# A two-layer decoder trunk on one core: every probability tile transposed by DMA, its halves parted and joined on ScalarE, VectorE and GpSimd

## The chip, the core and the metric

The kernel runs on one core of one Trainium2 chip. A core has TensorE (PE in the profile, with PEld for its weight loads), VectorE (DVE), ScalarE (ACT), GpSimd (POOL) and SyncE (SP, which only issues DMAs). Each engine executes its own instructions in a fixed order and waits for the others by semaphores. The metric is the time of one execution in device microseconds, lower is better.

## The reference

The input x is 256 tokens x 1024 features, float32. Two layers, each an attention mixer and a SwiGLU feed-forward of width 2816, with RMS norms between:

```python
for i in range(DEPTH):                       # DEPTH = 2
    if i % 2 == 0: h = h + dilated_mixer(rmsnorm(h, a_norm), a_w_in, a_w_out)
    else:          h = h + forgetting_mixer(rmsnorm(h, b_norm), b_w_in, b_f, b_w_out)
    h = h + swiglu(rmsnorm(h, ffn_norm[i]), ffn_w_gu[i], ffn_w_down[i])
return rmsnorm(h, final_norm)
```

The first attention (`dilated_mixer`) has 16 heads of 64 features and three groups of query, key and value projections: group 0 sees the last 128 tokens, groups 1 and 2 every 4th and every 16th token. The outputs of the three are mixed by their softmax denominators, which amounts to one softmax over all three groups' scores. The second (`forgetting_mixer`) is causal attention over all 256 tokens with a bias from a learned decay. In both, probabilities p and values v meet as `p @ v`.

## The kernel before

TensorE multiplies in a reduced-precision float32 format. Each operand is therefore kept as a high and a low part (ScalarE rounds the high part, VectorE subtracts it, `split` at L80 and L84), and `mm3` does every product as three matmuls (L203, L208). The weights come from HBM in pieces of 1024 columns (`raw`, issued by SP at L101), five in flight, and are split two units of work ahead of their use (`AHEAD = 2`).

A *unit* is one weight matrix of 1024 x 256 times all tokens: 48 matmuls of 256 columns or 24 of 512. Heads are worked in four *quads* (`hq`) of four heads, a quad as two *pairs* (`pr`) of two heads (`h`). The list `a_units` writes the order of the first attention's 36 units out by hand, `b_units` that of the second's 12. `later(i, fn, ...)` puts attention work behind unit i of the list, `due.pop` carries it out there; in the second attention a due time of i - 0.5 is the middle of unit i.

In the first attention a quad goes through `scores_0` and `scores_12` (matmuls into PSUM), `softmax_a`, a transposition of the probabilities (each tile `p` holds 128 queries x 640 keys), and `pv_a`, the products with the values. Quads 0 to 2 transpose with `turn_a`: GpSimd parts each float32 into its two 16-bit halves (L528), SP issues a DMA that transposes the 16-bit blocks (L530), ScalarE joins the halves (L531). Quad 3 uses `trans_a`: TensorE multiplies each 128 x 128 block by the identity (`transposed`, L301), and ScalarE or VectorE copies the result from PSUM (L306). In the second attention all quads use TensorE (`trans_b`, three groups of four blocks): `scores_b` behind unit j, `trans_b` one and a half units later, `pv_b` two units later, where the next quad's `scores_b` stands too. `out_proj` then multiplies the attention's output (`ot`) by the output matrix in *triples* (one `mm3` of 512 columns), for the first 128 tokens and then for the other 128, and takes in what is still due: quad 3's transposition after some triples, its products after more, and after them the triples that need them. The norm of the first 128 tokens (`residual`, `norm_t`) is worked beside the second 128's triples.

`first()` raises the priority of instructions when the order of each engine is laid down; `issue_after` ties that order to an instruction. Buffers are named by tags ("pt", "bias", "xn", "p", "h"), each with a fixed number of slots.

Of the kernel before, what the change touches and what calls it, by code (L numbers as in the profile page):

```python
# [17 lines left out]
P = 128  # L18
# [14 lines left out]
def trunk(ctx: ExitStack, tc: tile.TileContext, T, out):  # L33
# [222 lines left out]
    def v_tile(o=None, r=None):  # L256

        v = ap.tile([P, 512], F32, tag="v", name="v", bufs=7)
        with first():
            if r:  # L260
                for t in range(2):
                    s = slice(t * S, (t + 1) * S)
                    nc.scalar.activation(v[:, s], o[:, s], AF.Copy, scale=r[t])
            elif o is not None:
                nc.scalar.activation(v, o, AF.Copy)
        return v
# [27 lines left out]

    copied = {}

    def transposed(blocks, copy=nc.vector.tensor_copy, tag="tr", home="pt"):

        tr = psum(tag)
        for i, b in enumerate(blocks):  # L300
            nc.tensor.transpose(tr[:, i * P:(i + 1) * P], b, ident)  # L301
        n = len(blocks) * P
        bufs, cols = {"pt": (3, 640), "bias": (4, 6 * P)}[home]
        w = ap.tile([P, cols], F32, tag=home, name="pt", bufs=bufs)
        with first():
            copied["last"] = copy(w[:, :n], tr[:, :n])  # L306
        return w
# [157 lines left out]
    def scores_12(quad):  # L465

        sc = [psum("sc") for _ in range(2)]
# [42 lines left out]
    def trans_a(quad, pr):  # L510

        pt = quad["pt"]
        block = lambda h, i: pt[pr, h][:, i * P:(i + 1) * P]
        home = ("pt", "bias")[pr]
        quad["w", pr] = [transposed([block(h, 1 + qb) for h in range(2) for qb in range(2)], nc.scalar.copy, home=home),
                         transposed([block(h, 3) for h in range(2)], home=home),
                         transposed([block(h, b * 4) for h in range(2) for b in range(2)], nc.scalar.copy, "o", home)]

    def turn_a(quad, pr):

        quad["w", pr] = []
        bufs = {"pt": 3, "bias": 4}
        parts = lambda x: x[:, :640].bitcast(U16).rearrange("p (c t) -> p t c", t=2)
        for h in range(2):
            home = ("pt", "bias")[pr]
            w = ap.tile([P, 640 if home == "pt" else 6 * P], F32, tag=home, name="pt", bufs=bufs[home])
            split16 = w[:, :640].bitcast(U16)
            nc.gpsimd.tensor_copy(split16.rearrange("p (t c) -> p t c", t=2), parts(quad["pt"][pr, h]))  # L528
            turned = ap.tile([P, 6 * P], F32, tag="bias", name="turned", bufs=4)[:, :640].bitcast(U16)
            nc.sync.dma_start_transpose(turned.rearrange("p (g c) -> p g c", c=P), split16)  # L530
            nc.scalar.copy(parts(w), turned.rearrange("p (t c) -> p t c", t=2))  # L531
            quad["w", pr].append(w)

    def pv_a(quad, pr):
        vs, ws = quad["v"], quad["w", pr]
        o = psum("o")
        if len(ws) == 2:
            blocks = [w[:, :640].rearrange("p (i j) -> p i j", j=P) for w in ws]
            straight = lambda h: ws[h][:, P:3 * P]
            corner = lambda h: ws[h][:, 3 * P:4 * P]  # L540
            dilated = lambda h, a: blocks[h][:, 0:5:4, a * 32:a * 32 + 32]
        else:
            straight = lambda h: ws[0][:, h * S:(h + 1) * S]
            corner = lambda h: ws[1][:, h * P:(h + 1) * P]
            dilated = lambda h, a: halves(ws[2][:, h * S:(h + 1) * S], a)
        pv(o[:, :S], vs[0], 0, pr, straight, S, True, False)
        pv(o[:, P:S], vs[0], 1, pr, corner, P, False, False)
        halves = lambda x, a: x.rearrange("p (b n) -> p b n", b=2)[:, :, a * 32:a * 32 + 32]
        for a in range(4):
            pv(halves(o[:, :S], a), vs[1 + a % 2], a // 2, pr, lambda h: dilated(h, a), 64, False, a == 3)  # L550
# [10 lines left out]
    for i, (hq, g, w) in enumerate(a_units):  # L561
# [6 lines left out]
        if i != 3 and (w < 2 or g == 0 and hq > 1):  # L568
            o = psum("mm")
# [11 lines left out]
        if w < 2:  # L581
# [26 lines left out]
            if w == 1:  # L608

                j = i + (hq == 0)  # L610
                step = lambda hq: 9 * hq + 11 + 2 * (hq == 0)
                if g == 0:
                    later(step(hq - 1) + 2 if hq else j + 3, scores_0, quad)
                if g == 2:
                    later(j + 1, scores_12, quad)
                    later(j + 1, softmax_a, quad)
                    for pr in range(2):
                        if hq == 3:
                            later(step(hq) + pr, trans_a, quad, pr)
                        else:  # L620
                            later(j + 1, turn_a, quad, pr)
                    for pr in range(2):
                        later(step(hq) + 2, pv_a, quad, pr)
        elif g == 0 and hq > 1:
            for t in range(2):
                proj_tok(xt, wt, o[:, t * S:(t + 1) * S], t)
            quad["v"][0] = v_tile(o, r_a)
# [30 lines left out]
    def out_proj(nm, ot, h, grow, ks, done, banks):  # L658
# [3 lines left out]
        res = []  # L662

        def part(t, acc, nk):
            last = None
            for n, k in nk:
                c = (k % 2) * D + n * 512
                last = mm3(acc[n], both(ot, ALL, k, slice(t * P, (t + 1) * P)),
# [3 lines left out]
        def cols(ks):  # L672
            return [(n, k) for n in range(2) for k in ks]

        for t in range(2):
            acc = [psum(banks[t]) for _ in range(2)]
            if t == 0:

                nk = cols(range(ks))
                last = part(t, acc, nk[:done])  # L680
                nk = nk[done:]
                per = -(-len(nk) // (len(due) - 1))
                for i in sorted(due):
                    with tc.issue_after(last.ins):
                        for fn, a in due[i]:
                            fn(*a)
                    last = part(t, acc, nk[:per]) or last
                    nk = nk[per:]
                due.clear()
                part(t, acc, nk)  # L690
                last = part(t, acc, cols(range(ks, KT)))
            else:
                part(t, acc, cols(range(2)))
                with tc.issue_after(last.ins):
                    part(t, acc, cols(range(2, 6)))
                    norm_t(*res[0], grow, xt, 0)
                    part(t, acc, cols(range(6, KT)))
            res.append(residual(acc, h[t], f"h_{nm}{t}"))
# [114 lines left out]
    hs, xt = out_proj("a_out", ot, x, g_f, 6, 6, ("sc", "mm"))  # L813
# [73 lines left out]
    def scores_b(hq):  # L887
# [9 lines left out]
        for pr in range(2):  # L897
# [13 lines left out]
            release(added)  # L911
# [7 lines left out]
    def trans_b(hq):  # L919
        pt = bq[hq]["pt"]  # L920
        square = lambda pr: [pt[pr, h][:, qb * P:(qb + 1) * P] for h in range(2) for qb in range(2)]
        w = [transposed(square(0)), transposed([pt[pr, h][:, 2 * P:3 * P] for pr in range(2) for h in range(2)]),
# [216 lines left out]
```

## Time and profile before

| | |
|---|---|
| median of 3 runs | 736.82 us (735.57 to 736.84) |
| profiled execution | 736.1 us, its span 734.3 us |
| granted TensorE clock | 0.997 |
| PE busy | 726.4 us (99%) |
| DVE busy | 495.9 us (68%) |
| ACT busy | 388.7 us (53%) |
| POOL busy | 83.0 us (11%) |
| DMA | 141.93 MB, 193 GB/s on average |

The span runs from the first instruction's start to the last one's end. The first attention takes about the first 240 us of it, the first feed-forward the time to about 430, the second attention to about 540. In a row of the timeline stand start, duration, engine, source line, operation, output <- inputs, shape and how many like instructions are merged; in brackets the idle time before it and what ended it. In a row of groups stand the count, the busy time, the mean in ns, and the idle time before. Matmuls overlap, so what one of them costs is read from start to start, not from its duration.

### The profile page before, as it was taken

Reading aid. Unit: us, or ns where it says so; the run is one execution under the profiler, and the core shown is the slowest. Engines: PE = TensorE matmul, PEld = TensorE weight load, DVE = VectorE, ACT = ScalarE, POOL = GpSimd, SP = SyncE. Lnnn points to the kernel's source line nnn. Section 1 sums busy time; section 2 is a strip of 40 time slices with the busy share of each in tenths; the row PEclk is TensorE's granted clock in tenths of the full one; section 3 lists DMA queues with packets and bytes.
Section 4 is the critical chain, followed back from the end, with each engine's and each line's share of the span. In section 5 each row is a group of like instructions: output and inputs, shape, how many; then the busy total and the mean of one; then the engine's idle time right before and its main releaser. Section 6 shows DMA issues by size and latency. Waiting matters only on the chain.

```text
span 734.3 us, 14310 instructions
## 1 busy us (share of the span) xinstructions
PE 726.4 (99%) x5856; PEld 672.4 (92%) x5856; DVE 495.9 (68%) x762; ACT 388.7 (53%) x617; POOL 83.0 (11%) x118
## 2 busy tenths in 40 slices
PE   9999999999999999999999999999999999999996
PEld 7999989999988899999999989999889999999995
DVE  6997998998996775554555474576776554556533
ACT  7646747738445663444554453587475444545421
POOL 0600206007105000000000004110010000000001
PEclk9999999999999999999999999999999999999998
DMA  9865955956864376656567352874547656656601
GB/s 335 306 202 174 237 182 153 289 193 152 268 194 160 116 241 221 195 179 203 195 202 247 127 168 90 294 260 138 172 142 237 222 179 203 195 188 218 198 1 58
DMA packets 55042, 141.93 MB, mean 193 GB/s; under 512 B 20257, under 2 KB 21441, under 8 KB 54977
## 3 DMA queue, kind: packets, MB, share of 16 engines
q1 hardware_dynamic: 54832, 140.88, 59.4%
q8 instruction: 46, 0.75, 0.4%
q14 instruction: 20, 0.16, 0.1%
q10 hardware_dynamic: 144, 0.15, 0.1%
HBM read 136.00 MB, written 1.07 MB: 187 GB/s over the span
## 4 chain that ended last, share of the span: by engine, by line
PE 97%; DVE 1%; ACT 1%; POOL 0%; issue 0%; POOLq 0%; DVEq 0%; ACTq 0%
PE ps_mm L208 34%; PE ps_mm L203 17%; PE ps_tr L208 9%; PE ps_sc L208 8%; PE ps_o L208 7%; PE ps_tr L203 5%; PE ps_sc L203 4%; PE ps_o L203 4%; PE ps_o L313 2%; PE ps_sc L395 2%; PE ps_tr L196 1%; PE ps_tr L301 1%; PE ps_sc L476 1%; PE ps_o L322 1%; PE ps_sc L894 0%; PE ps_sc L458 0%
## 5 line engine op out<-in xcount | busy, mean ns | idle before, releaser
L80 ACT ACTIVATE wh<-raw 128x1024 fp32r<-128x1024 f32 x236 | 243.4, 1054 | 207.1 <-PE ps_tr L208 66.7
L84 DVE TENSOR_TENSOR wl<-raw,wh 128x1024 fp32r<-128x1024 f32 x236 | 288.3, 1242 | 82.6 <-ACT wh L80 82.4
L203 PE MATMUL ps_mm<-xt,wh 128*128 128x256 f32 x816 | 227.2, 279 | 0.2 <-ACT v L281 0.2
L208 PE MATMUL ps_mm<-xt,wl 128*128 128x256 f32 x816 | 226.0, 277 | 0.0
L208 PE MATMUL ps_mm<-xt,wh 128*128 128x256 f32 x816 | 226.0, 277 | 0.0
L203 PEld LDWEIGHTS ps_mm<-xt,wh 128*128 128x128 f32 x816 | 153.1, 188 | 2.2 <-issue 1.7
L208 PEld LDWEIGHTS ps_mm<-xt,wl 128*128 128x128 f32 x816 | 153.6, 188 | 0.1
L208 PEld LDWEIGHTS ps_mm<-xt,wh 128*128 128x128 f32 x816 | 153.4, 188 | 0.0
L208 PE MATMUL ps_tr<-xt,wh 128*128 128x256 f32 x304 | 83.9, 276 | 0.0
L208 PE MATMUL ps_tr<-xt,wl 128*128 128x256 f32 x304 | 83.9, 276 | 0.0
L203 PE MATMUL ps_tr<-xt,wh 128*128 128x256 f32 x304 | 83.7, 276 | 0.0
L730 DVE TENSOR_TENSOR sa<-ps_tr,sa 128x256 f32<-128x256 f32 x38 | 16.1, 424 | 73.5 <-PE ps_tr L208 73.5
L208 PEld LDWEIGHTS ps_tr<-xt,wh 128*128 128x128 f32 x304 | 57.1, 188 | 0.0
L208 PEld LDWEIGHTS ps_tr<-xt,wl 128*128 128x128 f32 x304 | 57.0, 188 | 0.0
L203 PEld LDWEIGHTS ps_tr<-xt,wh 128*128 128x128 f32 x304 | 57.0, 188 | 0.0
L203 PE MATMUL ps_mm<-wh,xt 128*128 128x512 f32 (+1 forms) x144 | 49.8, 346 | 0.0
L173 POOL TENSOR_SCALAR rs<-ssq 128x1 f32<-128x1 f32 x7 | 1.9, 271 | 420.6 <-ACT junk L182 420.6
L208 PE MATMUL ps_mm<-wl,xt 128*128 128x512 f32 (+1 forms) x149 | 49.1, 335 | 0.0
L208 PE MATMUL ps_mm<-wh,xt 128*128 128x512 f32 (+1 forms) x149 | 49.1, 335 | 0.0
L285 POOL COPY v<-v 32x256 f32<-32x256 f32 x64 | 40.5, 632 | 71.2 <-ACT v L281 68.6
L203 PE MATMUL ps_sc<-wh,ah 128*128 128x512 f32 x80 | 31.4, 392 | 0.0
L208 PE MATMUL ps_sc<-wl,ah 128*128 128x512 f32 (+1 forms) x82 | 31.3, 385 | 0.0
(232 smaller groups left out, 1113.6 us busy)
## 6 DMA issues: line engine op xcount, KB each, us to landing
raw<-in_gu SPq DMA_DIRECT2D x88, 512.0 KB, 4.8
raw<-in_a_in SPq DMA_DIRECT2D x68, 512.0 KB, 5.0
raw<-in_dn SPq DMA_DIRECT2D x44, 512.0 KB, 4.7
raw<-in_b_in SPq DMA_DIRECT2D x24, 512.0 KB, 5.0
raw<-in_a_out SPq DMA_DIRECT2D x8, 512.0 KB, 5.0
raw<-in_b_out SPq DMA_DIRECT2D x8, 512.0 KB, 4.4
bias<-sums SPq DMA_DIRECT2D x8, 384.0 KB, 6.6
grow<-in_norms SPq DMA_DIRECT2D x4, 512.0 KB, 5.7
```

Of the source, the lines that this page charges most:

```text
L80: a = nc.scalar.activation(view(hi), src, AF.Copy)
L84: return nc.vector.tensor_tensor(view(lo), src, view(hi).bitcast(F32), op=ALU.subtract)
L196: nc.tensor.transpose(tr[:, k * P:(k + 1) * P], xn[:, kk * P:(kk + 1) * P], ident)
L203: nc.tensor.matmul(o, sh, mh, start=start, stop=False)
L208: last = nc.tensor.matmul(o[:, u], s, m[:, u], start=False, stop=end and u.stop == n)
L285: nc.gpsimd.tensor_copy(v[1 + a % 2][n:n + 32, a // 2 * S:a // 2 * S + S], by_t[a * 32:a * 32 + 32, t, g])
L301: nc.tensor.transpose(tr[:, i * P:(i + 1) * P], b, ident)
L313: nc.tensor.matmul(o[h * HD:(h + 1) * HD], v[:, c:c + HD], w(h), start=start, stop=stop)
L322: nc.tensor.matmul(o[:, :n], mhalf.to_broadcast([P, P]), mhalf.to_broadcast([P, n]), start=True, stop=True)
L395: nc.tensor.matmul(lead[t], xt[y][:, k, t * P:(t + 1) * P], w[z][:, u], start=k + y + z == 0, stop=k == KT - 1 and z == 1)
L476: nc.tensor.matmul(sc[h][c, o:o + 64], q[HR[h], pr, qb * P + a * 32:qb * P + a * 32 + 32], k[HR[h], pr].rearrange("p (b n) -> p b n", b=2) ...
L730: nc.vector.tensor_tensor(a, u, sg, op=ALU.mult)
```

## The change

- Quad 3 of the first attention and all quads of the second take the DMA path; `trans_a`, `trans_b` and `transposed` are gone. For quad 3 of the first attention, pair 0 is parted on GpSimd and joined on ScalarE, pair 1 is parted and joined on VectorE. In the second attention one DMA turns a pair's two heads (1536 halves); pair 0 is parted on GpSimd, pair 1 on VectorE, and head 0 of each is joined on ScalarE, head 1 on VectorE.
- The parts and joins of all quads are now issued under `first()`.
- In the second attention `pv_b` of quads 0 and 1 comes half a unit later than before, quad 2 and 3's in the output projection; quad 3's `scores_b` comes half a unit earlier.
- In the first attention the group-0 values of quads 2 and 3 are projected together, as the last two units (24 matmuls of 512 columns each), and `pv_a` of quad 2 moves into the output projection with quad 3's. Quad 3's two scores stand together, in different PSUM banks.
- `out_proj` has one written order for both: of the first 128 tokens the triples of quads 0 and 1, then four triples of the other tokens, then quad 2's, then quad 3's; due work comes in after triples 4 and 16 (first attention) or 8 and 16 (second).
- `release` (weight splits held back behind the softmax) comes after pair 1, not after each pair; the splits that waited for a transposition's copy no longer do.

```diff
-        a_units += ([(0, 0, 2), (1, 0, 2)], v12, [(hq, 0, 2)] + v12, v12 + [(hq, 0, 2)])[hq]
+        a_units += ([(0, 0, 2), (1, 0, 2)], v12, v12, v12 + [(2, 0, 2), (3, 0, 2)])[hq]
...
-        sc = [psum("sc") for _ in range(2)]
+        sc = [psum("sc" if quad["hq"] < 3 else "o") for _ in range(2)]
...
+    def parted(x):
+        return x.bitcast(U16).rearrange("p (c t) -> p t c", t=2)
...
     def turn_a(quad, pr):
...
+        last = quad["hq"] == 3
+        if last and pr == 0:
+            quad["room"] = [(hrow(f"apart{h}")[:, :640], p_tile(640)) for h in range(2)]
         for h in range(2):
...
+                own = last and pr == 1
+                (nc.vector if own else nc.gpsimd).tensor_copy(apart.rearrange("p (t c) -> p t c", t=2), parted(p))
...
+                nc.sync.dma_start_transpose(turned.rearrange("p (g c) -> p g c", c=P), apart)
+                (nc.vector.tensor_copy if own else nc.scalar.copy)(parted(w), turned.rearrange("p (t c) -> p t c", t=2))
...
-                    later(step(hq - 1) + 2 if hq else j + 3, scores_0, quad)
+                    later((j + 3, 15, 22, 32)[hq], scores_0, quad)
...
-                        later(step(hq) + 2, pv_a, quad, pr)
+                        later((15, 22, 40, 41)[hq], pv_a, quad, pr)
...
+        cols = lambda t, *ks: [(t, n, k) for i in ks for n in range(2) for k in (2 * i, 2 * i + 1)]
+        head = cols(0, 0, 1) + cols(1, 0) + cols(0, 2)
+        last = None
+        for i, item in enumerate(head + [None]):
+            if i in at:
                 with tc.issue_after(last.ins):
+                    for fn, a in due.pop(min(due)):
+                        fn(*a)
+            if item:
+                last = part(item)
+        last = part(*cols(0, 3))
+        res = [residual(accs[0], h[0], f"h_{nm}0")]
+        with tc.issue_after(last.ins):
+            part(*cols(1, 1, 2))
+            norm_t(*res[0], grow, xt, 0)
+            part(*cols(1, 3))
...
-            release(added)
+            if pr:
+                release(added)
...
+    def turn_b(hq, pr):
+
+        b = bq[hq]
+        w = b["w", pr] = b["bias", pr] if hq == 3 else turn_tile()
+        apart = w.bitcast(U16).rearrange("p (h t c) -> p h t c", h=2, t=2)
+        for h in range(2):
+            with first():
+                (nc.gpsimd, nc.vector)[pr].tensor_copy(apart[:, h], parted(b["pt"][pr, h][:, :3 * P]))
+        with first():
+            turned = ap.tile([P, D], F32, tag="xn", name="turned", bufs=2)[:, :6 * P].bitcast(U16)
+            nc.sync.dma_start_transpose(turned.rearrange("p (g c) -> p g c", c=P), w.bitcast(U16))
+            turned = turned.rearrange("p (h t c) -> p h t c", h=2, t=2)
+            for h in range(2):
+                (nc.scalar.copy, nc.vector.tensor_copy)[h](parted(w[:, h * 3 * P:(h + 1) * 3 * P]), turned[:, h])
...
-                later(j, scores_b, hq)
+                later(j - (hq == 3) / 2, scores_b, hq)
+                for pr in range(2):
+                    later(j - (hq == 3) / 2, turn_b, hq, pr)
+                for pr in range(2):
+                    later((7.5, 9.5, 13, 14)[hq], pv_b, hq, pr)
...
-                later(j + 1.5, trans_b, hq)
-                for pr in range(2):
-                    later(j + 2, pv_b, hq, pr)
```

More of the change, by code (lines that the diff above doesn't have):

```diff
@@ L254, in p_tile, with v_tile @@
         return ap.tile([P, 640], dtype, tag="p", name=name, bufs=6)[:, :n]
-    def v_tile(o=None, r=None):
+    def v_tile(o=None):
         v = ap.tile([P, 512], F32, tag="v", name="v", bufs=7)
[L259 to L264, printed above, removed]
+        if o is not None:
+            with first():
                 nc.scalar.activation(v, o, AF.Copy)
@@ L293, in masked @@
             nc.vector.scalar_tensor_tensor(s, sc, HD ** -0.5, mask, op0=ALU.mult, op1=ALU.add)
[L295 to L307, printed above, removed]
     def pv(o, v, kb, pr, w, n, start, stop):
@@ L524, in turn_a @@
         for h in range(2):
[L525 to L530, printed above, removed]
@@ L531, in turn_a @@
-            nc.scalar.copy(parts(w), turned.rearrange("p (t c) -> p t c", t=2))
+            p = quad["pt"][pr, h]
+            with first():
+                apart, turned = quad["room"][h] if last else (home(("pt", "bias")[pr]), None)
+                w = p if last else apart
+                apart = apart.bitcast(U16)
+                own = last and pr == 1
+                (nc.vector if own else nc.gpsimd).tensor_copy(apart.rearrange("p (t c) -> p t c", t=2), parted(p))
+                if not last:
+                    turned = home(("bias", "pt")[pr * (h == 0)])
+                turned = turned.bitcast(U16)
+                nc.sync.dma_start_transpose(turned.rearrange("p (g c) -> p g c", c=P), apart)
+                (nc.vector.tensor_copy if own else nc.scalar.copy)(parted(w), turned.rearrange("p (t c) -> p t c", t=2))
@@ L567, in trunk @@
             wt = weights("a_in", hq * 9 + g * 3 + w, read if i > 4 else None)
-        if i != 3 and (w < 2 or g == 0 and hq > 1):
+        if i != 3 and w < 2:
             o = psum("mm")
@@ L617, in trunk @@
                     for pr in range(2):
[L618 to L621, printed above, removed]
+                        later(j + 1, turn_a, quad, pr)
                     for pr in range(2):
-                        later(step(hq) + 2, pv_a, quad, pr)
[L624 to L627, printed above, removed]
+                        later((15, 22, 40, 41)[hq], pv_a, quad, pr)
         elif i > 1:
@@ L656, in residual, with out_proj, part @@
         return hn, parts
-    def out_proj(nm, ot, h, grow, ks, done, banks):
+    def out_proj(nm, ot, h, grow, at, banks):
         ws = [weights(nm, i) for i in range(4)]
         xt = xt_tile()
-        res = []
-        def part(t, acc, nk):
+        accs = {}
+        def part(*items):
             last = None
-            for n, k in nk:
+            for t, n, k in items:
+                if t not in accs:
+                    accs[t] = [psum(banks[t]) for _ in range(2)]
                 c = (k % 2) * D + n * 512
-                last = mm3(acc[n], both(ot, ALL, k, slice(t * P, (t + 1) * P)),
+                last = mm3(accs[t][n], both(ot, ALL, k, slice(t * P, (t + 1) * P)),
@@ L699, in out_proj @@
+        res.append(residual(accs[1], h[1], f"h_{nm}1"))
         return res, xt
@@ L967, in trunk @@
             continue
-        lows = [] if any(fn is trans_b for fn, _ in due.get(i - 0.5, ())) else None
-        wt = weights("b_in", hq * 3 + w, behind if i in (3, 5) else lows, hold=held)
+        wt = weights("b_in", hq * 3 + w, behind if i in (3, 5) else None, hold=held)
         o = psum("mm")
@@ L976, in trunk @@
                         fn(*a)
-                    for low in lows or ():
-                        low(copied["last"])
             if w == 0:
@@ L1002, in trunk @@
                         fn(*a)
-                    for low in lows or ():
-                        low(copied["last"])
             bq[hq][w] = v_tile(o)
```

75 lines of the change are left out of this document (17 added, 58 removed).

## The prediction

> **What bounds the kernel now.** I read the page first: busy times, then the chain that ended last.
>
> ```profile
> span 734.3 us, 14310 instructions
> PE 726.4 (99%) x5856; PEld 672.4 (92%) x5856; DVE 495.9 (68%) x762; ACT 388.7 (53%) x617; POOL 83.0 (11%) x118
> PE 97%; DVE 1%; ACT 1%; POOL 0%; issue 0%; POOLq 0%; DVEq 0%; ACTq 0%
> ```
>
> TensorE is busy 99% of the span and is 97% of the chain, so a matmul taken away is time won, as long as nothing that replaces it makes TensorE wait. The profiled execution took 736.1 us, 0.7 below the median of 736.8; a change under 0.2% of that, 1.5 us, can't be told from none.
>
> The unit of cover is read from the timeline of PE: first and last of the 48 matmuls of one unit of 256 columns.
>
> ```profile
> 220.08 0.28 PE L203 MATMUL ps_mm<-wh,xt 128*128 128x256 f32 x1
> 225.41 0.28 PE L208 MATMUL ps_mm<-wh,xt 128*128 128x256 f32 x1
> ```
>
> 47 steps in 5.33 us are 0.113 us a matmul, 5.44 us a unit.
>
> **What goes: the transposes on TensorE.** The same timeline, one group of the first attention and the group of one head quad in the second:
>
> ```profile
> 229.63 0.81 PE L301 MATMUL ps_tr<-ident,p 128*128 128x128 f32 x6
> 230.29 0.60 PE L301 MATMUL ps_o<-ident,p 128*128 128x128 f32 x4
> 230.64 0.48 PE L203 MATMUL ps_sc<-wh,oth 128*128 128x512 f32 x1
> ...
> 525.60 1.03 PE L301 MATMUL ps_tr<-ident,p 128*128 128x128 f32 x8
> 526.47 0.60 PE L301 MATMUL ps_o<-ident,p 128*128 128x128 f32 x4
> 526.82 0.48 PE L203 MATMUL ps_mm<-wh,oth 128*128 128x512 f32 x1
> 527.14 0.40 PE L208 MATMUL ps_mm<-wl,oth 128*128 128x512 f32 x1
> 527.37 0.40 PE L208 MATMUL ps_mm<-wh,otl 128*128 128x512 f32 x1
> ```
>
> Start to start, a matmul of 512 columns takes 0.23 us (527.14 to 527.37), the first after a group 0.32. Ten transposes hold PE from 229.63 to 230.64, with 0.09 for the slow restart 1.10 us; twelve hold it from 525.60 to 526.82, with 0.09 1.31 us. Removed are two groups of ten (quad 3, first attention) and four of twelve: 2 x 1.10 + 4 x 1.31 = **7.44 us**.
>
> **What comes back on TensorE.** Before, a quad's products with the values stand right before the next quad's scores; half a unit later they are a stretch of their own. Three such joints are cut in the second attention. A stretch costs its entry and exit:
>
> ```profile
> 528.76 0.40 PE L208 MATMUL ps_mm<-wh,otl 128*128 128x512 f32 x1
> 529.09 1.52 PE L313 MATMUL ps_o<-pt,v 128*64 128x256 f32 x16
> 530.54 0.50 PE L203 MATMUL ps_mm<-wh,oth 128*128 128x512 f32 x1
> 530.87 0.40 PE L208 MATMUL ps_mm<-wl,oth 128*128 128x512 f32 x1
> ```
>
> 0.33 in place of 0.23 on both sides: 0.2 a stretch, **+0.6 us** for three (0 to 0.6, since two kinds of work side by side may cost a step too). In the first attention the count stays: quad 3's two scores are joined, quad 2's products are parted from them. The products themselves take 1.45 us as before. The values of group 0, quads 2 and 3, become 48 matmuls of 512 columns for 96 of 256: 48 x 0.23 against 96 x 0.113, both 10.9 us, nothing.
>
> **The new path of a probability tile** is part (copy by 16-bit halves), transpose on SP's queue, join (copy back). Three quads of the first attention take it already:
>
> ```profile
> L530 SPq DMA_TRANSPOSE turned<-pt x12: 1267/1366/1601, 73.8 to 185.0; - x12
> L531 ACT COPY pt<-turned x12: 1647/1672/1698, 77.5 to 188.5; 128x1280 uint16<-128x1280 uint16 x12
>   DMA turned<-pt: 14.5, 8
> DMA to landing us min/median/max: 3.3/3.5/5.8
> L528 POOL COPY pt<-p x12: 1247/1358/2245, 72.2 to 183.4; 128x1280 uint16<-128x1280 uint16 x12
> ```
>
> In the second attention one transfer holds two heads, 1536 halves, and each copy 768. By length: a part on POOL 0.6 x 1358 = 0.82 us, a join on ACT 1.0, the transfer 3.5 to 1.2 x 3.5 = 4.2, taken 3.9. A DVE copy of this kind isn't in the trace: 348 ns for 256 elements (row below) gives 1.04 for 768 as the high end, half of that the low one; I take 0.9 for the load and 0.8 in the chain. A handover adds 0.3.
>
> The trace says: landing 3.5 us. [...]
>
> **Is the path covered?** Quad 0 of the second attention has the longest softmax, quad 3 the shortest distance to the end. Chain view, then VectorE and ScalarE timelines:
>
> ```profile
> 472.17 0.66 PE ps_tr L894 x8
> 518.75 0.66 PE ps_tr L894 x8
> ...
> 479.41 0.61 DVE L916 TENSOR_SCALAR p<-p,c_b 128x256 f32<-128x256 f32 x2
> 525.48 0.62 DVE L916 TENSOR_SCALAR p<-p,c_b 128x256 f32<-128x256 f32 x2
> ...
> 479.80 0.68 ACT L915 ACTIVATE p<-p,c_b 128x128 f32<-128x128 f32 x2
> 481.34 0.68 ACT L915 ACTIVATE p<-p,c_b 128x128 f32<-128x128 f32 x2
> ```
>
> Quad 0: scores end at 472.83; pair 0 is ready 7.7 us later (480.48), pair 1 9.2 (482.02), perhaps 1.2 earlier because `release` no longer stands between the pairs. Pair 0: 7.7 + 1.6 + 3.9 + 0.3 + 1.0 = 14.5. Pair 1: 9.2 + 1.6 + 3.9 + 0.3 + 1.0 = 16.0. The products come after units 6 and 7, the next scores (1.5) and half of unit 8: 2.5 x 5.44 + 1.5 = 15.1, pair 1 another 0.7 later, 15.8. So a wait of 0.2, and with the transfer at its high end 0.5: **+0.4**. Quads 1 and 2 have 16.5 us and more. Quad 3: scores end 519.41, pair 1 ready 6.7 later (526.10), joined at 13.5; cover half a unit 2.7, sixteen column triples 16 x 0.68 = 10.9, quad 2's products 1.8: 15.4. Hidden, with 2 us left.
>
> Quad 3 of the first attention: its dilated scores take 1.6, then come 3 units (16.3), sixteen triples (10.9) and quad 2's products (2.38 in the chain and an entry, 2.7): 31.5 us of cover. Quad 2 needed, by the chain and the timeline of ACT,
>
> ```profile
> 158.25 1.41 PE ps_sc L476 x91
> 198.08 2.38 PE ps_o L313 x48
> ...
> 188.49 1.67 ACT L531 COPY pt<-turned 128x1280 uint16<-128x1280 uint16 x1 [6.85 <-DMA turned<-pt]
> ```
>
> 158.25 to 190.16, 31.9 us, with four parts on POOL among sixteen value copies; its products began at 198.08, so nothing waited. Quad 3 leaves two parts there and has two on VectorE, so I take it as hidden; 0.4 is the other end. Quad 2's products, moved behind all units, need nothing late but the values of the last unit, four triples (2.7 us) before.
>
> The output projections' order: after the last product of the first half, norm transposes have eight triples (5.4 us) of cover for twelve.
>
> ```profile
> 533.62 0.69 DVE L654 TENSOR_TENSOR h_b_out<-ps_mm,hf 128x512 f32<-128x512 f32 x1 [0.69 <-PE ps_mm L208]
> 536.08 1.41 DVE L191 SCALAR_TENSOR_TENSOR xn<-h_b_out,rs,grow 128x512 f32<-128x512 f32 x2 [0.70 <-POOL rs L176]
> ```
>
> That chain takes 533.62 to 537.49, 3.9 us: hidden, 1.5 left; without cover it would cost the difference. Weights are needed later than before there, which pays for VectorE's four added copies in quad 3.
>
> **Load of the copying engines**, second attention (stage table 470 to 530, its last line) and the groups of lines:
>
> ```profile
> sum 60.00, PE 60.00 PEld 54.57 DVE 44.71 ACT 42.49 POOL 5.83; mean PE 10.00 PEld 9.09 DVE 7.45 ACT 7.08 POOL 0.97
> ...
> L306 DVE COPY pt<-ps_tr 128x512 f32<-128x512 f32 x8 | 5.2, 686 | 6.1 <-PE ps_tr L301 6.0
> L916 DVE TENSOR_SCALAR p<-p,c_b 128x256 f32<-128x256 f32 x16 | 4.9, 348 | 0.1
> ```
>
> DVE loses 12 evictions (x 0.686 = 8.2; the row groups eight of them) and gains 8 parts and 8 joins (16 x 0.9 = 14.4): 50.9 us. ACT gains 8 joins: 50.5. POOL gains 8 parts, 6.6, and stays idle. PE's stretch becomes 60 - 5.2 + 0.6 = 55.4. Both copying engines go above 90%, and their queues stand still while a join at the head waits for its transfer: 14.5 us over 12 transfers before, 1.2 each, 9.7 for eight. 50.9 + 9.7 is 5.2 too much. The weights are split two units ahead (10.9 us), which absorbs it, but eviction and softmax lose some room: I take **+0.8** (0 to 5.2). Tightest is quad 3: its scores now stand in the middle of the last unit, so the eviction of its keys (512 columns, about the 0.69 of the L306 row) has half a unit, 2.7 us, instead of a whole one; a join at the head of ScalarE that waits over 2 us is paid by TensorE there. On SP the transfers hold back the weight loads behind them by up to their wait for a part; all of that lies in the same lead. `release` after pair 1 delays weight splits by four short VectorE operations, in the lead too.
>
> **Sum.** 736.1 - 7.44 + 0.6 + 0.4 + 0.8 = 730.5; against the median 731.2 us. One more uncertainty: ten microseconds of like matmuls hold 87 or 91 of them,
>
> ```profile
> 120.00:130.00 10.00, 10.00 (x87) 10.00 (x86) 10.00 (x14) 7.96 (x9) 8.06 (x8) 1.00 0.55 102
> 180.00:190.00 10.00, 10.00 (x91) 10.00 (x90) 9.80 (x13) 3.15 (x3) 6.03 (x7) 1.00 0.44 116
> ```
>
> at a full granted clock (1.00) with no wait; 4% over some 30 us, so +-1 us if it changes.
>
> **Rivals.** *The queues don't absorb it* (chance 0.16): the 5.2 us above falls on TensorE in full. 736.8 - 6.8 + 5.2 = 735.2, or anything between. For it: 91% load. Against: the first attention has DVE at 10.00 of 10 in the rows above and PE never stops.
>
> *VectorE stands behind its joins* (slower, 0.13). Its eight joins each hold the queue for a transfer that is late because SP was behind a blocked weight load. With 55.4 - 50.9 + 10.9 = 15.4 us of room, it decides from 1.9 us a join; at 4 us, 32 - 15 = 17 us stall: 736.8 - 6.8 + 17 = 747. It is slower than before from 2.8 us a join ((15.4 + 6.8) / 8). For it: a wait of 6.85 in the row above. Against: the mean of 1.2. GpSimd's parts push the same way: weight splits took
>
> ```profile
> 165.81 1.19 DVE L84 TENSOR_TENSOR wl<-raw,wh 128x1024 fp32r<-128x1024 f32 x1
> 170.88 3.87 DVE L84 TENSOR_TENSOR wl<-raw,wh 128x1024 fp32r<-128x1024 f32 x2 [0.85 <-ACT wh L80]
> ```
>
> 1.94 us each beside POOL copies, 1.19 without. [...]
>
> *Hidden anyway* (0.07): gains and waits cancel within 0.2%, 735.3 to 738.3. Against: PE's transposes are on the chain.
>
> **How the numbers follow.** My forecast of 729 to 733 has 0.64, a part of the 5.2 us (733 to 735.3) 0.16; together faster 0.80, same 0.07, slower 0.13. Low end: all waits 0, no new stretches, matmul pace 1 us better: 736.8 - 7.4 - 1 = 728.4. High end: the first rival in full, 735.2, and the pace 1 us worse: 736.2. Between them lie some 8 in 10.
>
> **What would show it.** No L301 rows; PE busy some 6 us less; around each quad's products no PE gap above 0.5 us. Wrong if PE waits for a join (DVE or ACT, `pt<-turned`) before L313, or if weight splits come late to L203 in the second attention; if DVE's 768 copies take over 1.04 us; or if landings rise above 4.2.

## The result and the profile after

The changed kernel takes 747.01 us (median of four runs; the kernel before, timed beside it, 736.2): ratio 1.0148, 95% interval 1.0126 to 1.0169. The forecast was 731.2, the range 728.4 to 736.2; the sign was wrong. The profiled execution took 745.77 us. Its page, the lines that answer to those of before:

```profile
span 743.8 us, 14168 instructions
PE 724.7 (97%) x5742; PEld 665.5 (89%) x5742; DVE 505.9 (68%) x768; ACT 396.6 (53%) x623; POOL 89.0 (12%) x128
PE 72%; DVE 11%; ACT 5%; DMA 5%; issue 4%; POOL 1%; POOLq 0%; SPq 0%; DVEq 0%; ACTq 0%
```

The transposes are gone, but TensorE is 72% of the chain and not 97%: it waits now. The table by stage shows where. First before, then after; the rows are the first attention and the second, the columns window, length, busy time of PE, PEld, DVE, ACT and POOL, granted clock, DMA share, GB/s:

```profile
50.00:250.00 200.00, 199.82 (x2042) 183.01 (x2041) 171.41 (x266) 119.11 (x180) 47.58 (x62) 1.00 0.63 191
470.00:550.00 80.00, 80.00 (x601) 71.00 (x600) 59.15 (x143) 56.00 (x132) 8.22 (x17) 1.00 0.58 194
```

```profile
50.00:250.00 200.00, 196.88 (x1968) 177.69 (x1968) 176.34 (x268) 119.79 (x178) 46.97 (x64) 1.00 0.67 200
470.00:550.00 80.00, 71.71 (x520) 61.80 (x519) 55.56 (x138) 55.40 (x129) 13.67 (x24) 0.96 0.84 219
```

TensorE idles 2.9 us more in the first attention (199.82 - 196.88) and 8.3 in the second (80.00 - 71.71); there the clock of 0.96 over 71.71 busy us takes another 2.9. Together 14.1, against the 7.44 - 0.6 = 6.84 us that were to be won: +7.3. The spans differ by 9.5; 2.2 us are not placed by this sum. VectorE was not fuller: in the second attention it was busy for 55.56 us, before for 59.15.

Who is waited for, in the list of TensorE's waits (total, times, longest):

```profile
PE ps_sc L203 <- DVE nm_b L869: 3.6, 1, 3.6
PE ps_o L295 <- ACT pt L896: 3.2, 2, 2.7
PE ps_o L295 <- issue: 1.5, 1, 1.5
PE ps_mm L203 <- DVE fm L425: 0.9, 2, 0.7
```

The second row is a wait for joins ahead of the products, which was foreseen as what would show the forecast wrong. The first row is something else: the output projection's first triple waits for a PSUM bank that quad 3's scores hold until VectorE has read them (`nm_b`, L869). VectorE's timeline says why it is late:

```profile
521.12 0.61 DVE L896 COPY pt<-turned 128x768 uint16<-128x768 uint16 x1 [2.71 <-DMA turned<-pt]
521.63 1.21 DVE L84 TENSOR_TENSOR wl<-raw,wh 128x1024 fp32r<-128x1024 f32 x1
522.75 0.59 DVE L896 COPY pt<-turned 128x768 uint16<-128x768 uint16 x1
523.24 1.21 DVE L84 TENSOR_TENSOR wl<-raw,wh 128x1024 fp32r<-128x1024 f32 x1
524.37 0.28 DVE L869 CUSTOM_DVE_ANT_0 p<-ps_sc,bias 128x128 f32<-128x128 f32 x1
```

A join of quad 2 stands at the head for 2.71 us until its transfer lands, and quad 3's softmax, whose scores TensorE had finished at 518.5, stands behind it, a second join and two splits. TensorE had no other work from 521.5 on; it restarts at 525.05, and then runs at half pace for a while (its timeline; the granted clock from 520 to 530 was 0.83):

```profile
525.05 0.50 PE L203 MATMUL ps_sc<-wh,oth 128*128 128x512 f32 x1 [3.58 <-DVE nm_b L869]
525.64 0.63 PE L208 MATMUL ps_sc<-wh,otl 128*128 128x512 f32 x1
526.07 0.63 PE L203 MATMUL ps_sc<-wh,oth 128*128 128x512 f32 x1
...
528.63 0.57 PE L203 MATMUL ps_sc<-wh,oth 128*128 128x512 f32 x1
```

From 525.64 to 528.63 a step is 0.43 us, not 0.23: seven steps, with the two at the edges some 1.6 us. The wait ahead of them is 3.58 us. After the shorter wait of 2.66 us before quad 1's products (the longest of the second row) the pace halves too: the steps are 0.21 us for 256 columns in place of 0.113, from 510.7 to 511.8. The last section has shorter waits still.

The transfers of the second attention, in the view of the tile `turned`, 470 to 545:

```profile
L896 ACT COPY pt<-turned x6: 1034/1060/1085, 487.4 to 523.0; 128x768 uint16<-128x768 uint16 x6
L896 DVE COPY pt<-turned x6: 591/608/622, 487.4 to 522.8; 128x768 uint16<-128x768 uint16 x6
DMA to landing us min/median/max: 3.7/4.6/7.0
```

They land after 4.6 us in the median and 7.0 at worst, where 3.9 was taken. 393 KB in 4.6 us are 85 GB/s; in the trace of before 328 KB in 3.5 us were 94. VectorE's copies are cheaper than taken, 0.61 us for 0.9.

### The profile page after: what moved, and what is told of

It reads as the page before. It is cut to its first block, busy times and chain, and to the rows that moved or that the text cites. A ratio compares the mean times of both kernels' runs of the same rounds, so it can differ in the third digit from the quotient of the medians.

```text
span 743.8 us, 14168 instructions
## 1 busy us (share of the span) xinstructions
PE 724.7 (97%) x5742; PEld 665.5 (89%) x5742; DVE 505.9 (68%) x768; ACT 396.6 (53%) x623; POOL 89.0 (12%) x128
## 3 DMA queue, kind: packets, MB, share of 16 engines
HBM read 136.00 MB, written 1.07 MB: 184 GB/s over the span
## 4 chain that ended last, share of the span: by engine, by line
PE 72%; DVE 11%; ACT 5%; DMA 5%; issue 4%; POOL 1%; POOLq 0%; SPq 0%; DVEq 0%; ACTq 0%
PE ps_mm L208 20%; PE ps_mm L203 10%; PE ps_tr L208 9%; PE ps_o L208 8%; PE ps_sc L208 7%; PE ps_tr L203 5%; PE ps_o L203 4%; DVE wl L84 4%; PE ps_sc L203 4%; DMA turned<-pt 2%; PE ps_sc L377 2%; ACT wh L80 1%; DVE rt L424 1%; ACT p L285 1%; DVE rt L426 1%
## 5 line engine op out<-in xcount | busy, mean ns | idle before, releaser
L84 DVE TENSOR_TENSOR wl<-raw,wh 128x1024 fp32r<-128x1024 f32 x236 | 291.0, 1252 | 85.7 <-ACT wh L80 85.3
L281 POOL COPY v<-v 32x256 f32<-32x256 f32 x64 | 35.6, 557 | 110.7 <-ACT v L277 108.1
L203 PE MATMUL ps_mm<-wh,xt 128*128 128x512 f32 (+1 forms) x112 | 41.1, 367 | 0.7 <-DVE fm L425 0.7
L208 PE MATMUL ps_mm<-wh,xt 128*128 128x512 f32 (+1 forms) x117 | 40.3, 351 | 0.0
L208 PE MATMUL ps_mm<-wl,xt 128*128 128x512 f32 (+1 forms) x117 | 40.2, 351 | 0.0
```

The lines of the kernel that those rows point to most:

```text
L84: return nc.vector.tensor_tensor(view(lo), src, view(hi).bitcast(F32), op=ALU.subtract)
L203: nc.tensor.matmul(o, sh, mh, start=start, stop=False)
L208: last = nc.tensor.matmul(o[:, u], s, m[:, u], start=False, stop=end and u.stop == n)
L281: nc.gpsimd.tensor_copy(v[1 + a % 2][n:n + 32, a // 2 * S:a // 2 * S + S], by_t[a * 32:a * 32 + 32, t, g])
```

## The experiments

Three theories were tried. **Q** (queues): joins at the head of VectorE's and ScalarE's queues stand until their transfer lands, and hold back the next quad's softmax and the evictions. **L** (landing): the transfers are simply later than the cover before the products, wherever the joins stand. **C** (copies): the copying engines have too much work. The experiments are called e1 to e18. The kernel before, timed beside them, took 735.8 to 736.9 us (medians); each ratio is to it.

**Which half (e1, e2).** The first attention's functions, lists and `out_proj` from one kernel, the second's from the other:

```diff
 e1: a_units, turn_a, pv_a, out_proj("a_out", ...)  as changed;  trans_b, pv_b, out_proj("b_out", ...)  as before
 e2: a_units, trans_a, pv_a, out_proj("a_out", ...)  as before;  turn_b, pv_b, out_proj("b_out", ...)  as changed
```

> Only the first attention's part of the change (quad 3 by DMA, its values and products moved), the second attention with TensorE transposes as before. Takes away 2 x 1.10 = 2.2 us of transposes; the gaps of PE that the changed kernel shows in its first attention add up to 3.7 us. If those gaps belong to this half (theories Q, L and C agree): 736.8 - 2.2 + 3.7 = 738.3, ratio near 1.002. If they are brought on by the second attention's code: 734.6, ratio 0.997.

> Only the second attention's part (all four quads by DMA, products half a unit later, banks and order of its output projection), the first attention as before. Takes away 4 x 1.31 = 5.2 us; the gaps of PE in the changed kernel's second attention are 11.5 us. All three theories: about 743, ratio 1.008. Below 738 would mean that the loss is made in the first attention and only shows later.

e1 took 739.07 us, ratio 1.0038 (1.0023 to 1.0053); e2 741.59, 1.0071 (1.0056 to 1.0086). Each half loses by itself; the sum, +1.1%, is a little less than the +1.5% of both.

**Transfers or copies (e3), place of the joins (e4).**

```diff
 e3, turn_b:
-            nc.sync.dma_start_transpose(turned.rearrange("p (g c) -> p g c", c=P), w.bitcast(U16))
 (the parts write `turned`, the joins read it)
 e4, turn_b:
-                (nc.scalar.copy, nc.vector.tensor_copy)[h](parted(w[:, ...]), turned[:, h])
+                nc.gpsimd.tensor_copy(parted(w[:, ...]), turned[:, h])
```

> The changed kernel, but in the second attention the eight DMA transposes are left out: the parts write straight into the tile that the joins read, so its probabilities are not transposed; copies, queues' order and products are all there. Theories Q (late transfers hold the queues of VectorE and ScalarE, and the next softmax stands behind) and L (transfers are later than the cover before the products): the 11.5 us of gaps in the second attention go, 747 - 11.5 = 735.5. Theory C (the copies themselves are too much for VectorE and ScalarE): stays above 742.

> The changed kernel, with all joins of the second attention on GpSimd, which has few instructions there; transfers as they were. Theory Q: VectorE and ScalarE no longer stand, the wait of 3.75 us at the output projection's first triple and the 1.6 us of slow matmuls after it go, waits before the products stay: 738 to 742. Theory L: place in the queue does not matter and GpSimd's copies of 0.8 us each, one after the other, come later than before: 747 or more. Theory C: VectorE and ScalarE lose 8 us of copies, near 738 and without waits before the products.

e3 took 737.54 us, 1.0012 (1.0001 to 1.0023); only its times are used. Without the transfers, 9.5 us of the loss go, with all copies in place: C as the main cause is out, though 2 us of the 11.5 expected stay. Q and L are not told apart by it. e4 741.60, 1.0074 (1.0055 to 1.0093), where Q had 738 to 742. No wait of TensorE for a bank is left, and the products wait for GpSimd instead (another 1.2 us for quad 3's):

```profile
PE ps_o L295 <- POOL pt L896: 2.9, 4, 1.1
```

**Another bank, more cover (e5, e6).**

```diff
 e5, e6:
-    hs, xt = out_proj("b_out", ot, [h for h, _ in hs], g_f, (8, 16), ("sc", "mm"))
+    hs, xt = out_proj("b_out", ot, [h for h, _ in hs], g_f, (8, 16), ("mm", "sc"))
 e6 also:
-                    later((7.5, 9.5, 13, 14)[hq], pv_b, hq, pr)
+                    later((8, 10, 13, 14)[hq], pv_b, hq, pr)
```

> The changed kernel, only the banks of the second attention's output projection in the order that the kernel before has: its first row block in the mm pair, not in the sc pair that quad 3's scores hold. If the wait of 3.75 us before the first triple and the 1.6 us of slow matmuls after it are the price of that bank (theory Q: the softmax that frees it stands behind joins), they go: 747.0 - 5.3 = 741.7, between 740 and 743. If something else is just as late there (the last values' eviction, the products of quad 2 after eight triples), the wait only moves and it stays at 745 or more.

> As the one with the banks changed back, and the products of quads 0 and 1 another half unit later (after unit 8 and after unit 10), 2.7 us more cover. Theory L for the rest: the waits before the products (0.8, 3.8 and 0.5 us in the changed kernel) go, 741.7 - 4.7 = 737.0. If these waits are not set by how far off the products stand but by joins that are held up themselves (ScalarE and VectorE stand longer), half of it or more stays: 739 or more.

Both missed Q's and L's figures: e5 749.06 us, 1.0170 (1.0138 to 1.0203), e6 747.58, 1.0144 (1.0119 to 1.0169). What came is e5's other case, that something else is just as late there. TensorE's waits in e5, then in e6:

```profile
PE ps_mm L203 <- ACT v L261: 7.0, 1, 7.0
```

```profile
PE ps_mm L203 <- ACT v L261: 3.8, 1, 3.8
PE ps_sc L857 <- ACT fb L954: 3.8, 1, 3.8
```

The mm bank waits for the last values' eviction, which stands in ScalarE's queue behind two joins of quad 2 and quad 3's exponentials, as the softmax stands in VectorE's. In e6 no product of the second attention waits for a join any more (3.1 us in e5); yet the time is only 1.5 us below e5's, within the two intervals, and quad 3's scores now wait 3.8 us for the eviction of its keys (L954). Cover before the products alone is not what is short, which speaks against L.

**The order of one queue (e11, e13).** Quad 2's joins behind quad 3's softmax, asked for by the place in the program (e11), then bound on each engine (e13):

```diff
 e11:
+                if hq == 3:
+                    for pr in range(2):
+                        later(j - 0.5, join_b, 2, pr, True)       # behind scores_b(3); the parts and the transfer stay
 e13, join_b of quad 2 (late = the exponential and the reading of quad 3's scores):
+                with behind_(late[h]):
                     (nc.scalar.copy, nc.vector.tensor_copy)[h](parted(w[:, ...]), turned[:, h])
```

> The changed kernel with one order changed: quad 2's joins are issued behind quad 3's scores and softmax, not ahead of them; same engines, same copies, same transfers. Theory Q: quad 3's softmax frees its banks in time, the wait of 3.75 us at the output projection's first triple and the slow matmuls behind it (1.6) go; quad 2's products may then wait for their own joins, by 2 us at most: 741.7 to 744. If the transfer's landing or the copies' load set that wait, and not the place in the queue: 746 or more.

> The changed kernel with quad 2's joins bound behind quad 3's softmax on each engine: VectorE's behind its last reading of quad 3's scores, ScalarE's behind the last exponential of pair 0. In e11 the same was asked for, but one join of each engine still stood ahead. Theory Q: the wait at the output projection's first triple (3.1 us in e11, 3.6 in the changed kernel) goes and the slow matmuls behind it too; quad 2's products may wait 1 us: 741 to 743. If the wait is not made by the joins' place: 746 or more.

e11 took 747.10 us, 1.0142 (1.0122 to 1.0162): nothing is won, because VectorE's order still had a join ahead:

```profile
520.90 0.62 DVE L902 COPY pt<-turned 128x768 uint16<-128x768 uint16 x1 [2.42 <-DMA turned<-pt]
...
523.68 0.28 DVE L869 CUSTOM_DVE_ANT_0 p<-ps_sc,bias 128x128 f32<-128x128 f32 x1
```

e13, with the order bound, took 744.79 us, 1.0105 (1.0091 to 1.0120). On VectorE the joins come after the readings, and do not stand:

```profile
523.57 0.28 DVE L869 CUSTOM_DVE_ANT_0 p<-ps_sc,bias 128x128 f32<-128x128 f32 x1
...
525.89 0.58 DVE L906 COPY pt<-turned 128x768 uint16<-128x768 uint16 x1
```

TensorE's waits in e13's second attention:

```profile
PE ps_o L295 <- ACT pt L906: 3.0, 3, 2.0
PE ps_sc L203 <- ACT oth L80: 2.0, 2, 1.4
```

No wait for a bank is left; 470 to 550 has 74.99 us of PE busy at a clock of 0.98, for 71.71 at 0.96. From quad 0's first score (476.21 us, 472.50 in the changed kernel) to the end of the span it takes 266.6 us, 4.7 less than the changed kernel's 271.3. That is Q, shown for this wait. The second row is the same thing at another place (see e7). The whole gained only 2.2 us and missed the 741 to 743 expected. In the profiled executions TensorE idled 2.6 us more in the first attention of e13 (194.24 busy of 200), where code and order of every engine are the same as in the changed kernel; that difference has no explanation here.

**Joins on GpSimd and later products (e7), their order (e9, e14).**

```diff
 e7 = e2, and
-                (nc.scalar.copy, nc.vector.tensor_copy)[h](parted(w[:, ...]), turned[:, h])
+                (nc.gpsimd.tensor_copy if hq < 3 else (nc.scalar.copy, nc.vector.tensor_copy)[h])(parted(w[:, ...]), turned[:, h])
-                    later((7.5, 9.5, 13, 14)[hq], pv_b, hq, pr)
+                    later((8, 10, 13, 14)[hq], pv_b, hq, pr)
 e9 = e7, and
+                        later(13, join_b, 3, pr, True)      # behind pv_b of quad 2
 e14 = e9, and the joins of quad 3 under
+                with behind_(late[h]):                      # late = the two splits of quad 2's output
```

> The first attention as before the change; in the second all probabilities by DMA, with the joins of quads 0 to 2 on GpSimd, those of quad 3 on ScalarE and VectorE, and the products of quads 0 and 1 half a unit later than in the change. Takes away 5.2 us of transposes, adds 0.6 for stretches, and with no wait left but about 1 us for quad 3: 736.3 - 5.2 + 0.6 + 1 = 732.7, ratio 0.995. Theory C (copying engines too full): 737 or more.

> As e7 (first attention as before, joins of quads 0 to 2 on GpSimd, products later), with quad 3's joins issued behind the splits of quad 2's output and not ahead of them. In e7 TensorE waited 2.4 us for ScalarE's rounding of quad 2's output, which stood behind a join of quad 3. Theory Q: that wait goes, 737.8 - 2.4 = 735.4. If ScalarE was merely full: 737 to 738.

> As e9, with quad 3's joins bound behind the splits of quad 2's output on ScalarE and VectorE; in e9 they still stood ahead of them and TensorE waited 2.4 us for the rounded output. Theory Q: that wait goes, some tenths come back before quad 3's own products: 738.5 - 2.4 + 0.5 = 736.6, ratio 1.000. If ScalarE was merely full: 738 or more.

e7 took 737.80 us, 1.0020 (1.0003 to 1.0036); e9 738.96, 1.0035 (1.0024 to 1.0047); e14 737.47, 1.0009 (0.9995 to 1.0022). All three are slower than Q's figures (732.7, 735.4, 736.6); e7 by its time alone lies where the text on record put C. e9 is e11's miss again: ScalarE's order kept the joins ahead.

```profile
527.91 1.05 ACT L980 COPY bias<-turned 128x768 uint16<-128x768 uint16 x1 [3.42 <-DMA turned<-bias]
...
530.15 0.63 ACT L80 ACTIVATE oth<-ps_o 128x256 fp32r<-128x256 f32 x2
```

TensorE waited 2.2 us for that rounding in e7 and 2.4 in e9; in e14, with the order bound, the row is gone from its waits. So Q holds at a second place, the end of the second attention. By the time it is worth 1.5 us against e9; e14 and e7 can't be told apart, and e14 still waits 0.8 us for the low part of an output (L84) and 0.8 for GpSimd's joins.

**More cover for quads 0 and 1 (e10, e18), one join on ScalarE (e17).**

```diff
-                    later((8, 10, 13, 14)[hq], pv_b, hq, pr)
+                    later((8.5, 10.5, 13, 14)[hq], pv_b, hq, pr)                                # e10 (on e9)
+                    later((8, 10, 13, 14)[hq] + (pr / 2 if hq < 2 else 0), pv_b, hq, pr)        # e18 (on e14)
 e17 (on e14), turn_b: quads 0 and 1, pair 1, second head joined by nc.scalar.copy
```

> As e9, and the products of quads 0 and 1 another half unit later (inside units 9 and 11). In e7 they waited 1.36 + 0.46 + 0.78 us for GpSimd's joins, and ran about 1 us longer than before for it. All waits gone: 735.4 - 2.6 - 1 = 731.8, ratio 0.994, faster than both kernels. If the joins of quad 1 or 2 then wait for buffers that the products free later: 734 or more.

> As e14, with the products of pair 1 of quads 0 and 1 half a unit later than those of pair 0. The waits there (0.55 + 0.46 + 0.78 us above a step) and the slow matmuls behind them (about 1 us) go, two more stretches cost 0.4: 737.5 - 2.8 + 0.4 = 735.1, ratio 0.998. If pair 0 then waits in the same way or a load gets between two transfers, as in e10: 738 or more.

> As e14, with the last join of quads 0 and 1 (pair 1, second head) on ScalarE in place of GpSimd. Lands 1.07 us sooner at the products: the same waits go, 737.5 - 2.5 = 735.0. Theory Q sees a price: ScalarE stands for the transfer again, and in quad 1 one weight load is now issued between the two transfers, so that the second lands after 6 to 7 us in place of 4 to 5: 738 to 742.

e10 took 744.47 us, 1.0110 (1.0094 to 1.0126), where 731.8 was hoped for: SP's order changed with the products. e10's SP queue, then e9's, at quad 1's two transfers:

```profile
499.76 1.44 SPq L971 DMA_TRANSPOSE turned<-pt  x1
501.29 1.33 SPq L101 DMA_DIRECT2D raw<-in_b_out  x2
502.71 2.43 SPq L971 DMA_TRANSPOSE turned<-pt  x1
```

```profile
500.97 3.29 SPq L971 DMA_TRANSPOSE turned<-pt  x2
```

With weight loads between them the second transfer is late: it landed after 6.8 us, the first after 3.7. TensorE then waits 4.4 us for GpSimd's joins, and 4.2 us at the end for the rounding of quad 2's output behind quad 3's join. The slowest transfer of the changed kernel (7.0) stands in the same way, behind a load issued 0.6 us before it:

```profile
499.97 0.53 SPq L101 DMA_DIRECT2D raw<-in_b_out  x1
500.60 2.13 SPq L893 DMA_TRANSPOSE turned<-pt  x1
```

e18 took 737.62 us, 1.0022 (1.0008 to 1.0035), for 735.1 hoped: the waits for GpSimd are gone, but 1.3 and 0.8 us before the last triples, for the splits of quad 3's output, are in its list, and its clock from 470 to 550 is 0.98. e17 took 738.75, 1.0033 (1.0019 to 1.0046), within the price that Q saw: ScalarE stands again, here before quad 1's last join, whose transfer landed after 5.3 us behind a load. Quad 2's softmax and the eviction of quad 3's keys (L1041, at 510.10 in e14) come later for it, and TensorE waits 2.5 us for that eviction.

```profile
504.42 1.07 ACT L982 COPY pt<-turned 128x768 uint16<-128x768 uint16 x1 [4.65 <-DMA turned<-pt]
...
512.76 0.57 ACT L1041 ACTIVATE fb<-ps_mm 128x512 f32<-128x512 f32 x1
```

**The size of a transfer (e12).**

```diff
-            nc.sync.dma_start_transpose(turned.rearrange("p (g c) -> p g c", c=P), w.bitcast(U16))
+            for h in range(2):
+                half = slice(h * 6 * P, (h + 1) * 6 * P)
+                nc.sync.dma_start_transpose(turned[:, half].rearrange("p (g c) -> p g c", c=P), w.bitcast(U16)[:, half])
```

> The changed kernel with each transfer of the second attention cut in two, one head (768 halves, 197 KB) each: 16 in place of 8. If a transfer's time goes with its size (theory: bandwidth), the first half lands after about half of 4.6 us, 2.3 to 2.8, its join starts sooner and holds its queue less: 744 or less. If most of it is a fixed time (1280 halves took 3.5 us and 1536 took 4.6), each half takes 3 us or more, and with twice as many on one queue it comes out at 747 to 750.

e12 took 746.00 us, 1.0121 (1.0096 to 1.0146), between the two cases. Its sixteen transfers:

```profile
DMA to landing us min/median/max: 2.8/3.7/4.8
```

Half the bytes take 3.7 us in the median for 4.6, and 2.8 at best for 3.7, though each second half stands behind the first: most of a transfer's time does not go with its size.

**The first attention (e8, e15, e16).**

```diff
 e8 = the changed first attention, e7's second, and
-    hs, xt = out_proj("a_out", ot, x, g_f, (4, 16), ("sc", "mm"))
+    hs, xt = out_proj("a_out", ot, x, g_f, (8, 16), ("sc", "mm"))
-            with first():                                   # turn_a
+            with (first() if last else nullcontext()):
 e15 = before, and
-                            later(step(hq) + pr, trans_a, quad, pr)
+                            later(j + 1, turn_a, quad, pr)  # quad 3 parted and joined as in the change, products after 12 triples
 e16 = e15's first attention and e14's second
```

> The second attention as in e7; the first attention as in the change, but quad 2's products after eight column triples and not after four (2.7 us more cover), and the parts of quads 0 to 2 without the raised priority that the change gave them. If the 1.6 us before quad 2's products are cover alone they go, and if the priority caused the gaps behind rotations (0.8 + 0.4 + 0.9) they go as well: 732.7 - 2.2 + 0.5 = 731.0. If the rotations are late because values of group 0 of quads 2 and 3 moved to the end and bring rotations closer together, 2 us of gaps stay: 733.

> The kernel before, with only quad 3's probabilities of the first attention through DMA (parts on GpSimd and VectorE, joins on ScalarE and VectorE); its values, products and the order of units stay as before, the second attention too. Takes away two groups of ten transposes, 2.2 us. If the loss of the first attention comes with the moved values and products (theory: rotations closer together, quad 2's values late): 736.4 - 2.2 = 734.2, ratio 0.997. If the DMA path of quad 3 costs it: 737 or more.

> The first attention of e15 and the second of e14. The sum of their differences: with theory Q for both, 736.4 - 2.2 + 0.2 = 734.4, ratio 0.997, faster than both kernels; if neither holds, 739 or more.

e8 took 739.33 us, 1.0037 (1.0022 to 1.0052); e15 740.84, 1.0050 (1.0036 to 1.0065); e16 739.45, 1.0039 (1.0025 to 1.0053). All three missed the gain that was hoped for (731.0, 734.2, 734.4). e8's waits in the first attention, then e15's:

```profile
PE ps_mm L203 <- DVE fm L425: 1.5, 3, 1.0
```

```profile
PE ps_o L313 <- DVE p L533: 2.8, 1, 2.8
```

Four more triples of cover took away the 1.5 us before quad 2's products (no such row in e8). Without the raised priority every engine's order in the first attention is the same as in the changed kernel, and the waits for rotations (L425) stayed, so the priority is not their cause. In e15, which keeps the order of units, there are none, so they come with what was moved, the values of group 0 or quad 3's scores; which of the two is not shown. But e15 pays elsewhere: quad 3's products wait 2.8 us for VectorE's joins, whose transfer landed after 6.4 us behind two weight loads, and the products after the wait take 3.4 us where the pair before took 1.3 (granted clock 0.66 from 239 to 244). Both parts of the change cost there; the DMA path alone is no gain even with some 22 us between scores and products.

No version was faster than the kernel before. The best, e14, cannot be told from it. How the changed kernel's loss divides between Q and late landings is not settled to the microsecond: the two feed each other, as quad 1 shows below.

## Why the prediction was wrong, by its own steps

- **The 7.44 us.** Their rows are gone. They were not won, because the chain no longer is TensorE alone. TensorE's busy time fell by 1.7 us only (726.4 to 724.7), where some 6 were forecast; 2.9 of the difference is the lower clock after the waits, a term that the forecast does not have.
- **The transfer, 3.9 us** (3.5 to 4.2): measured 4.6, up to 7.0 behind a weight load. The step scaled the median of a row whose longest landing, 5.8, it left aside. In the trace of before, ten of the twelve transfers landed after 3.3 to 3.7 us; the two that were issued 1.1 and 1.6 us after a weight load took 5.4 and 5.8. The second of them:

```profile
128.43 0.64 SPq L101 DMA_DIRECT2D raw<-in_a_in  x1
130.05 1.27 SPq L530 DMA_TRANSPOSE turned<-pt  x1
```

  In the forecast's sum the loads only wait for the transfers; that a transfer may be late behind a load stands in a rival alone. The 0.3 of handover was about right for the whole path: quad 2's pair 0 lost 0.22 us from softmax to part (514.40 to 514.62), 0.03 from part to transfer (516.21 to 516.24) and some 0.1 from landing (516.24 + 4.8) to join (521.11).
- **Quads 1 and 2 "have 16.5 us and more".** Quad 1's products waited 2.7 us. Its pair 1 was only sent at 500.60, against an estimate of 10.8 us after the scores (about 498), and then took the 7.0. It was sent late because its softmax began late, behind a join of quad 0 on VectorE; its scores were done at 487.0:

```profile
490.29 0.61 DVE L896 COPY pt<-turned 128x768 uint16<-128x768 uint16 x1 [2.21 <-DMA turned<-pt]
490.79 0.28 DVE L869 CUSTOM_DVE_ANT_0 p<-ps_sc,bias 128x128 f32<-128x128 f32 x1
```

  Quad 0 waited 0.56 us, near the 0.2 to 0.5 forecast, with some luck: its pair 1 was joined 17.2 us after the scores and not 16.0, but the products too came 1 us later than counted.
- **The load of the engines, +0.8.** This is the step that failed most. It compared sums over 60 us: work, plus standing time, against room. The changed kernel's waits, 470 to 545:

```profile
ACT pt L896 <- DMA turned<-pt: 12.9, 5, 3.2
DVE pt L896 <- DMA turned<-pt: 8.4, 5, 2.7
ACT bias L896 <- DMA turned<-bias: 3.7, 2, 2.1
DVE bias L896 <- DMA turned<-bias: 2.1, 2, 1.4
```

  VectorE stood 8.4 + 2.1 us for its eight joins, 1.3 a join, under the 1.9 from which the slower rival was to decide; ScalarE stood 12.9 + 3.7. And VectorE's own work was smaller than counted: its joins took 0.61 us, not 0.9. By the sum nothing was to be lost. The rival names what happened, a join that holds VectorE's queue behind a late transfer; but its 747 us were worked out for 4 us a join, so that this figure is met is luck. What failed is the step from sums to time: weight splits have a lead of two units, but the next quad's softmax and the evictions, right behind the waiting join, have far less.
- **The bank, put at nothing.** The output projection's first rows now use the sc banks, which quad 3's scores hold. The prediction does not have this wait. It named another as the tightest, the eviction of quad 3's keys behind a join on ScalarE; that one cost 0.2 us (`PE ps_sc L857 <- ACT fb L954`). The bank came through VectorE and cost 3.6 us, and the slow matmuls after it 1.6.
- **Quad 2's products in the first attention "need nothing late but the values".** These were late, 1.5 us (the row with `issue` above): ScalarE's timeline has joins and splits ahead of their eviction, the four copies from 228.50.

```profile
223.58 3.20 ACT L517 COPY p<-p 128x1280 uint16<-128x1280 uint16 x2 [2.10 <-DMA p<-apart]
226.60 2.02 ACT L80 ACTIVATE wh<-raw 128x1024 fp32r<-128x1024 f32 x2
228.50 1.59 ACT L268 ACTIVATE v<-ps_o,rs_a 128x256 f32<-128x256 f32 x4
```

- **Right:** quad 3's path of the first attention was covered at the products, and VectorE's copies stayed below the high end (0.61).
- **Right by luck:** quad 3's products of the second attention did not wait either. But the joins were done at 539.3, 20.8 us after its scores and not 13.5, where the cover was put at 15.4; what covered them is TensorE's own delay at the bank (3.6 + 1.6).

## What to carry over

Where a copy waits for a DMA, ask what its engine has queued right behind it, and who waits for that; a sum of busy times does not answer it. Put such copies on an engine with nothing urgent behind them, or bind them behind the urgent work on that very engine, and read the order that came out, since a place in the program is only a wish. And ask what the DMA has in front of it on its queue.

## What was not expected of the hardware

- A transposing transfer issued close behind a weight load on SP's queue lands late. At 0.5 to 0.6 us behind a load, transfers landed after 7.0 us (changed kernel), 6.8 and 6.4 (e10); at 0.8 to 1.6 us behind one, after 4.8 to 6.4 (before, changed kernel, e2, e15, e17). With no load in the 4 us ahead they landed after 3.3 to 4.4 (before, changed kernel, e2, e10, e14, e17), with one exception of 5.1. Why is not shown. Half as many bytes landed after 3.7 in the median (e12).
- How long TensorE waits does not by itself tell whether its pace halves. After a wait of 2.0 us it did in e13: steps of 0.21 us for 256 columns from 513.08 on, where 0.113 is usual, until 515.9 (below). In e18 waits of 1.3 and 0.8 us, one soon after the other, were followed by steps of 0.43 us for 512 columns (granted clock from 470 to 550: 0.98; 1.00 in e14, with waits of 1.0 and 0.8). But in e9 a wait of 2.4 us and in e11 one of 2.8 were followed by steps of 0.23 to 0.24 us for 512 columns, the full pace, and in e7, with a wait of 2.2, the granted clock from 520 to 540 was 1.00. e13's timeline of PE:

```profile
511.80 0.97 PE L295 MATMUL ps_o<-pt,v 128*64 128x256 f32 x8 [2.02 <-ACT pt L906]
...
513.08 0.42 PE L208 MATMUL ps_mm<-xt,wh 128*128 128x256 f32 x1
513.30 0.41 PE L208 MATMUL ps_mm<-xt,wl 128*128 128x256 f32 x1
```
- A join of 768 halves: VectorE 0.61 us, ScalarE 1.06 (changed kernel); GpSimd 1.07 in e4.
